# A two-layer hybrid decoder trunk: another opening order in the mixer, another order of the three passes, constant products at the start, the last scalings on one engine

## The chip, the cores and the metric

The kernel runs on one core of a Trainium2 chip. Work is done by TensorE (PE, matrix products, with a separate row PEld for loading its stationary operand), VectorE (DVE), ScalarE (ACT) and GpSimd (POOL); SyncE (SP) issues nearly all transfers. Each engine takes its instructions in the order in which they were written, and waits on semaphores for the others.

The metric is the device time of one execution in microseconds (us); less is better. Times "in the trace" count from the start of the profiled span.

## The reference

Two layers over a sequence of 512 positions of width 1024, float32. Each layer adds half of a gated feed-forward block, then a mixer of two branches (an attention in "stick-breaking" form with 4 heads of 128, and a state-space model with 24 heads of 64), then half of a second feed-forward block. A normalisation stands ahead of every block and at the end.

```python
for l in range(DEPTH):
    x = x + 0.5 * swiglu(rms_norm(x, ffn1_norm[l]), ffn1_w_up[l], ffn1_w_down[l])
    h = rms_norm(x, mix_norm[l])
    proj = h @ w_in[l]
    q, k, v, z, xbc, dt_raw, gate_sb, gate_ssm = jnp.split(proj, IN_SPLITS, axis=-1)
    y_sb = stick_breaking_attention(q, k, v) @ w_branch_sb[l]
    y_ssm = mamba2_mixer(z, xbc, dt_raw, ...) @ w_branch_ssm[l]
    merged = jax.nn.sigmoid(gate_sb) * y_sb + jax.nn.sigmoid(gate_ssm) * y_ssm
    x = x + merged @ w_out[l]
    x = x + 0.5 * swiglu(rms_norm(x, ffn2_norm[l]), ffn2_w_up[l], ffn2_w_down[l])
return rms_norm(x, final_norm)
```

The attention scores of a query block come from q and k; v enters only in the last product of a head.

## The kernel before

**Layout.** The activations stand transposed: the width of 1024 is cut into 8 blocks of 128 partitions, each 512 positions long (tiles of 128x512). A product of such an input with one weight "unit" (8 blocks of 128x128, 512 KB) gives one 128x512 result in a PSUM tile `mm`.

**Products in three passes.** Inputs and weights are float32 and are split into a high and a low part of the type float32r (hi + lo). `mm3` (L219) multiplies hi by hi, then the weight's hi by the input's lo, then the weight's lo by the input's hi, all into the same PSUM tile. `dense` (L225) does this for the 8 blocks of a unit: 8 triples, 24 products. In the rows of a profile or of an order, `mm<-hlo,whi` is a product whose moving operand is the input's low part `hlo` and whose stationary operand is the weight's high part `whi`.

**Weights.** `fetch` (L178) loads a unit into one of three raw buffers, `convert` (L184) makes the high part on ScalarE and the low part on VectorE (`wlo`, L199; for the first two units on GpSimd). `unit_order` (L77) lists the units in the order in which they are used; `unit` (L202) starts the conversion two units ahead.

**Order of the work.** The program is written by hand as one stream. Each dense triple ends in a `tick` (L153), which advances all side tasks (generators) that are due; a `yield n` in a side task says how many ticks later it goes on. So what an engine does, and in which order, is fixed when the program is built.

**Norms without waiting.** A block of the network starts with products of the input that is not yet scaled by its norm, since the norm needs the sum of squares over all 8 blocks: `norm_square` (L340) squares on ScalarE and adds on VectorE or GpSimd, `norm_end` (L357) sums over partitions with a product by ones (L363) on TensorE, and the scale `rs` follows on ScalarE and VectorE. Results of unscaled products ("not normed") are multiplied by `rs` afterwards (`scaled`, L376). Meanwhile `scale_blocks` (L260) scales the input blocks on VectorE (L265), and at one unit `project(..., swap=True)` (L238) makes the new high and low parts of the scaled input (`swapped`, L251; low part at L257); all later products use those.

**The opening of the mixer** (`mixer`, L862): the first three units are q, k and v of head 0, all from the unscaled input, with the swap at the third. Then, for each head, `qkv` (L526) starts a side task `qkv_parts` (L533) for each of the three results and one for `attention` (L561). `qkv_parts` scales an unscaled result into a tile `raw`; for v it then transposes it on TensorE (`transposed`, L518, products with the identity into a PSUM tile `pt`), and splits the result into a high and a low part (tiles `yt`). A scaled q or k is split straight from PSUM. `attention` begins with the score products of q and k (tile `pa`), which read the split parts. The heads follow as q, k, v.

**The ends.** `build` (L957) loads the first weight unit and the 8 input blocks, sets the constants, and starts. At its end the 8 blocks are scaled by the last `rs` (L999), three of them on GpSimd and five on VectorE, and stored (L1000).

Of the kernel before, what the change touches and what calls it, by code (L numbers as in the profile page):

```python
# [11 lines left out]
ALU = mybir.AluOpType  # L12
# [4 lines left out]
P = 128  # L17
SEQ = 512
NT = SEQ // P
DM = 1024  # L20
KB = DM // P
DEPTH = 2
SBH = 4
# [52 lines left out]

def unit_order(layer):  # L77
# [44 lines left out]
class Builder:  # L122
# [96 lines left out]
    def mm3(self, ps, a, b, start, stop, **kw):  # L219
        mm = self.nc.tensor.matmul  # L220
        mm(ps, a[0], b[0], start=start, stop=False, **kw)  # L221
        mm(ps, a[0], b[1], start=False, stop=False, **kw)  # L222
        mm(ps, a[1], b[0], start=False, stop=stop, **kw)  # L223
# [302 lines left out]
    def qkv(self, layer, h, first):  # L526
        parts = {}
        for t in "qkv":
            ps, normed = first[t] if first is not None else self.project(layer, t, h)
            self.spawn(self.qkv_parts(t, ps, normed, parts))  # L530
        self.spawn(self.attention(h, parts))

    def qkv_parts(self, t, ps, normed, parts):  # L533
# [11 lines left out]
        yield 2  # L545
# [316 lines left out]
    def mixer(self, layer):  # L862
# [4 lines left out]
        first = {}  # L867
        for t in "qkv":
            while t == "v" and self.scaled_blocks < KB // 2:
                self.tick()  # L870
            first[t] = self.project(layer, t, 0, swap=t == "v")
        xd, self.xd = self.xd, None
        self.xpool.__exit__(None, None, None)
        with ExitStack() as mix:
# [17 lines left out]
            with tc.tile_pool(name=f"mp{layer}", bufs=2, reuse_waits="tile") as self.mp:  # L892
# [64 lines left out]
    def build(self):  # L957
# [15 lines left out]
        self.consts()  # L973
        self.norm_start()
# [18 lines left out]
        with tc.tile_pool(name="fin", bufs=KB, reuse_waits="tile") as self.fin:  # L993
            self.xg = []
            self.ffn(DEPTH - 1, 2, self.pars[DEPTH - 1][:, G_FFN2:G_FFN2 + KB], None)
            self.flush()
            for m in range(KB):
                eng = nc.gpsimd if m in (1, 4, 7) else nc.vector
                eng.tensor_tensor(self.xg[m], self.xg[m], self.rs, op=ALU.mult)  # L999
                nc.sync.dma_start(self.out[m], self.xg[m])  # L1000
# [102 lines left out]
```

## Time and profile before

| | |
|---|---|
| device time, median of 3 runs | 2706.88 us (2706.11 to 2707.74) |
| the profiled execution | 2707.11 us, its span 2705.3 us |
| mean granted TensorE clock | 0.995 |
| busy: TensorE, VectorE, ScalarE, GpSimd | 2659.8, 1361.5, 1098.8, 316.2 us |
| moved to and from HBM | 261.43 MB read, 12.68 MB written |

How to read rows of the profile: in the timeline a row has the start, the duration, the engine, the line of the kernel, the operation, output<-inputs, the shape, the count of merged instructions, and in brackets the idle time before it with what ended it. In a list of waits a row has who waited for whom, the total, how often and the longest. In a table of windows a row has the window, its length, the busy time (and instructions) of PE, PEld, DVE, ACT and POOL, the granted TensorE clock, the share of the DMA engines and the GB/s. Products are pipelined: a row shows 0.39 us for one, while the next starts 0.23 us after it.

### The profile page before, as it was taken

Reading aid. Unit: us, or ns where it says so; the run is one execution under the profiler, and the core shown is the slowest. Engines: PE = TensorE matmul, PEld = TensorE weight load, DVE = VectorE, ACT = ScalarE, POOL = GpSimd, SP = SyncE. Lnnn points to the kernel's source line nnn. Section 1 sums busy time; section 2 is a strip of 40 time slices with the busy share of each in tenths; the row PEclk is TensorE's granted clock in tenths of the full one; section 3 lists DMA queues with packets and bytes.
Section 4 is the critical chain, followed back from the end, with each engine's and each line's share of the span. In section 5 each row is a group of like instructions: output and inputs, shape, how many; then the busy total and the mean of one; then the engine's idle time right before and its main releaser. Section 6 shows DMA issues by size and latency. Waiting matters only on the chain.

```text
span 2705.3 us, 31140 instructions
## 1 busy us (share of the span) xinstructions
PE 2659.8 (98%) x12248; PEld 2209.4 (82%) x12248; DVE 1361.5 (50%) x1933; ACT 1098.8 (41%) x1825; POOL 316.2 (12%) x479
## 2 busy tenths in 40 slices
PE   8999999999999999999999999999999999999997
PEld 6888878888888888888878888788888888788886
DVE  6333375565665464333553333755666745733333
ACT  5222246655564243222432223566555543422223
POOL 1000011132232010000100000112232410100001
PEclk9999999999999999999999999999999999999999
DMA  4322242233324423322232322323333243222322
GB/s 141 101 94 98 90 126 72 90 113 108 107 95 131 137 86 102 100 95 99 89 101 95 99 95 95 117 72 106 104 112 109 95 137 119 95 100 95 100 92 72
DMA packets 85539, 276.14 MB, mean 102 GB/s; under 512 B 10080, under 2 KB 10336, under 8 KB 85392
## 3 DMA queue, kind: packets, MB, share of 16 engines
q1 hardware_dynamic: 85104, 274.08, 30.9%
q8 instruction: 96, 1.57, 0.2%
q14 instruction: 51, 0.42, 0.1%
q10 hardware_dynamic: 288, 0.07, 0.0%
HBM read 261.43 MB, written 12.68 MB: 101 GB/s over the span
## 4 chain that ended last, share of the span: by engine, by line
PE 91%; DVE 6%; ACT 2%; issue 1%; DMA 0%; POOL 0%; DVEq 0%; SPq 0%; ACTq 0%
PE mm L221 28%; PE mm L222 28%; PE mm L223 28%; PE pt L523 1%; PE pa L765 1%; DVE wlo L199 1%; DVE tt L265 1%; DVE hlo L257 1%; PE pa L603 1%; PE pa L767 1%; PE pt L750 1%; ACT whi L195 1%; DVE cv L667 1%; PE pt L748 1%; DVE x L265 0%
## 5 line engine op out<-in xcount | busy, mean ns | idle before, releaser
L221 PE MATMUL mm<-hhi,whi 128*128 128x512 f32 x2512 | 1003.9, 400 | 6.2 <-ACT hhi L335 6.2
L222 PE MATMUL mm<-hlo,whi 128*128 128x512 f32 x2512 | 982.5, 391 | 7.0 <-DVE hlo L257 6.8
L223 PE MATMUL mm<-hhi,wlo 128*128 128x512 f32 x2512 | 982.7, 391 | 0.0
L195 ACT CAST whi<-wraw 128x1024 fp32r<-128x1024 f32 (+2 forms) x476 | 476.2, 1001 | 842.1 <-PE mm L222 517.1
L199 DVE TENSOR_TENSOR wlo<-wraw,whi 128x1024 fp32r<-128x1024 f32 (+2 forms) x472 | 586.6, 1243 | 393.5 <-ACT whi L195 392.6
L222 PEld LDWEIGHTS mm<-hlo,whi 128*128 128x128 f32 x2512 | 474.1, 189 | 105.3 <-DVE hlo L257 11.0
L223 PEld LDWEIGHTS mm<-hhi,wlo 128*128 128x128 f32 x2512 | 473.1, 188 | 100.8
L221 PEld LDWEIGHTS mm<-hhi,whi 128*128 128x128 f32 x2512 | 474.0, 189 | 98.7 <-ACT hhi L335 6.2
L223 PE MATMUL mm<-act,wlo 128*128 128x512 f32 x704 | 274.0, 389 | 0.0
L222 PE MATMUL mm<-act,whi 128*128 128x512 f32 x704 | 274.0, 389 | 0.0
L221 PE MATMUL mm<-act,whi 128*128 128x512 f32 x704 | 274.0, 389 | 0.0
L355 POOL TENSOR_TENSOR acc<-acc,sq 128x512 f32<-128x512 f32 x36 | 47.8, 1328 | 1551.9 <-ACT sq L348 1551.9
L412 DVE SCALAR_TENSOR_TENSOR x<-mm,x 128x512 f32<-128x512 f32 x96 | 66.1, 689 | 230.9 <-PE mm L223 230.9
L390 ACT ACTIVATE g<-mm 128x512 f32<-128x512 f32 x79 | 47.2, 598 | 311.2 <-PE mm L223 311.2
L404 DVE TENSOR_TENSOR a<-mm,g 128x512 f32<-128x512 f32 x88 | 60.7, 690 | 209.6 <-PE mm L223 209.6
L667 DVE SCALAR_TENSOR_TENSOR cv<-mm,conv,cv 128x511 f32<-128x511 f32 (+2 forms) x192 | 142.6, 743 | 34.8 <-ACT cv L664 33.2
L223 PEld LDWEIGHTS mm<-act,wlo 128*128 128x128 f32 x704 | 132.2, 188 | 27.5
L222 PEld LDWEIGHTS mm<-act,whi 128*128 128x128 f32 x704 | 132.2, 188 | 27.4
L221 PEld LDWEIGHTS mm<-act,whi 128*128 128x128 f32 x704 | 132.2, 188 | 27.3
L283 DVE TENSOR_TENSOR act<-a,act 128x512 fp32r<-128x512 f32 x88 | 60.9, 692 | 60.3 <-ACT act L278 60.3
L737 ACT ACTIVATE dec<-cumb,tok 128x128 f32<-128x128 f32 x192 | 62.9, 392 | 38.9 <-PE pa L765 38.9
L221 PE MATMUL mm<-yt,whi 128*128 128x512 f32 x192 | 74.9, 390 | 0.0
(208 smaller groups left out, 2451.4 us busy)
## 6 DMA issues: line engine op xcount, KB each, us to landing
wraw<-in_wflat_dram SPq DMA_DIRECT2D x394, 512.0 KB, 3.3
wraw<-in_wflat_dram SPq DMA_DIRECT2D x64, 384.0 KB, 3.1
cumb<-cum_d SPq DMA_DIRECT2D x16, 768.0 KB, 4.1
xd<-x SPq DMA_DIRECT2D x16, 256.0 KB, 4.0
wraw<-in_wflat_dram SPq DMA_DIRECT2D x16, 256.0 KB, 3.1
x<-xd SPq DMA_DIRECT2D x16, 256.0 KB, 5.2
gd<-gs SPq DMA_DIRECT2D x12, 256.0 KB, 2.1
gd<-gm SPq DMA_DIRECT2D x12, 256.0 KB, 2.0
```

The costliest lines, as they stand in the source:

```text
L195: nc.scalar.copy(hi[:, ps], raw[:, ps])
L199: eng.tensor_tensor(lo[:, ps], raw[:, ps], hi[:, ps].bitcast(F32), op=ALU.subtract)
L221: mm(ps, a[0], b[0], start=start, stop=False, **kw)
L222: mm(ps, a[0], b[1], start=False, stop=False, **kw)
L223: mm(ps, a[1], b[0], start=False, stop=stop, **kw)
L283: self.nc.vector.tensor_tensor(lo, src, hi.bitcast(F32), op=ALU.subtract)
L355: eng.tensor_tensor(self.acc, self.acc, sq, op=ALU.add)
L390: nc.scalar.activation(g, pg, AF.Silu)
L404: self.nc.vector.tensor_tensor(a, pu, g, op=ALU.mult)
L412: self.nc.vector.scalar_tensor_tensor(x, pd, 0.5, x, op0=ALU.mult, op1=ALU.add)
L667: nc.vector.scalar_tensor_tensor(u[:, i:], ps[:, :SEQ - i], tap[KCONV - 1 - i], u[:, i:], op0=ALU.mult, op1=ALU.add)
L737: nc.scalar.activation(dec[:, i, :], cumb[:, i, span(c)], AF.Relu, scale=-1.0, bias=tok[:, c, 32 + h0 + i:33 + h0 + i])
```

## The change

Four edits:

1. `qkv_order`, a new function, sets the order of the projections: q0, k0, q1, v0, k1, v1, then q, k, v of heads 2 and 3, with `dt` after head 2. The first three, from the unscaled input, are now q0, k0, q1; the swap is at q1. v0 comes fourth, from the scaled input, and is copied on ScalarE instead of scaled. The weights are laid out in that order.
2. For every v the transposes come four ticks after the result is in `raw` instead of two.
3. `mm3` multiplies by the input's low part last.
4. Eleven products of the constant `ones` with itself (128x128, into a PSUM tile nobody reads) stand ahead of the first norm, and all eight last scalings are on VectorE.

```diff
+def qkv_order():
+    yield from (("q", 0), ("k", 0), ("q", 1), ("v", 0), ("k", 1), ("v", 1))
+    for h in range(2, SBH):
+        yield from (("q", h), ("k", h), ("v", h))
+        if h == SBH - 2:
+            yield "dt", None
@@ unit_order
-    for h in range(SBH):
-        for t in "qkv":
-            yield (layer, t, h), KB
-        if h == SBH - 2:
-            yield (layer, "dt"), KB
+    for t, h in qkv_order():
+        yield ((layer, "dt") if t == "dt" else (layer, t, h)), KB
@@ mm3
         mm(ps, a[0], b[0], start=start, stop=False, **kw)
-        mm(ps, a[0], b[1], start=False, stop=False, **kw)
-        mm(ps, a[1], b[0], start=False, stop=stop, **kw)
+        mm(ps, a[1], b[0], start=False, stop=False, **kw)
+        mm(ps, a[0], b[1], start=False, stop=stop, **kw)
@@ qkv_parts (the function qkv is gone)
-        yield 2
+        yield 4 if t == "v" else 2
@@ mixer
-        first = {}
-        for t in "qkv":
-            while t == "v" and self.scaled_blocks < KB // 2:
+        first = []
+        order = list(qkv_order())
+        for i in range(3):
+            while i == 2 and self.scaled_blocks < KB // 2:
                 self.tick()
-            first[t] = self.project(layer, t, 0, swap=t == "v")
+            first.append(self.project(layer, *order[i], swap=i == 2))
...
-                for h in range(SBH):
-                    self.qkv(layer, h, first if h == 0 else None)
-                    if h == SBH - 2:
+                parts = [{} for _ in range(SBH)]
+                for i, (t, h) in enumerate(order):
+                    if t == "dt":
                         self.spawn(self.dt_stage(layer, self.project(layer, "dt")[0]))
+                        continue
+                    ps, normed = first[i] if i < len(first) else self.project(layer, t, h)
+                    self.spawn(self.qkv_parts(t, ps, normed, parts[h]))
+                    if t == "k":
+                        self.spawn(self.attention(h, parts[h]))
@@ build
+        warm = self.t(self.ptr, [P, SEQ], "pt")
+        for _ in range(11):
+            nc.tensor.matmul(warm[:, :P], self.ones, self.ones, start=True, stop=True)
         self.norm_start()
...
-                eng = nc.gpsimd if m in (1, 4, 7) else nc.vector
-                eng.tensor_tensor(self.xg[m], self.xg[m], self.rs, op=ALU.mult)
+                nc.vector.tensor_tensor(self.xg[m], self.xg[m], self.rs, op=ALU.mult)
```

The order of instructions shows where this lands. First TensorE at the very start, before:

```order
L221 MATMUL mm_186<-hhi_133,whi_130 128x512
L222 MATMUL mm_186<-hlo_134,whi_130 128x512
L223 MATMUL mm_186<-hhi_133,wlo_131 128x512
L221 MATMUL mm_186<-hhi_140,whi_130 128x512
L222 MATMUL mm_186<-hlo_141,whi_130 128x512
L223 MATMUL mm_186<-hhi_140,wlo_131 128x512
```

and now (L227 to L229 are the three passes of the changed kernel):

```order
L981 MATMUL pt_130<-ones 128x128 x11
L227 MATMUL mm_198<-hhi_145,whi_142 128x512
L228 MATMUL mm_198<-hhi_145,wlo_143 128x512
L229 MATMUL mm_198<-hlo_146,whi_142 128x512
L227 MATMUL mm_198<-hhi_152,whi_142 128x512
L228 MATMUL mm_198<-hhi_152,wlo_143 128x512
L229 MATMUL mm_198<-hlo_153,whi_142 128x512
```

The constant products come first, and in each triple the product with `hlo` has moved from second to last.

Second, TensorE in the opening of the mixer of layer 0, in the fourth unit (before: q1; now: v0), from the third triple to the first score product `pa`; `pt<-ident,raw` are the transposes of v0. Before:

```order
L223 MATMUL mm_2764<-hhi_2708,wlo_2645 128x512
L523 MATMUL pt_2791<-ident,raw_2774 128x128 x4
L221 MATMUL mm_2764<-hhi_2717,whi_2644 128x512
L222 MATMUL mm_2764<-hlo_2718,whi_2644 128x512
L223 MATMUL mm_2764<-hhi_2717,wlo_2645 128x512
L221 MATMUL mm_2764<-hhi_2724,whi_2644 128x512
L222 MATMUL mm_2764<-hlo_2725,whi_2644 128x512
L223 MATMUL mm_2764<-hhi_2724,wlo_2645 128x512
L221 MATMUL mm_2764<-hhi_2731,whi_2644 128x512
L222 MATMUL mm_2764<-hlo_2732,whi_2644 128x512
L223 MATMUL mm_2764<-hhi_2731,wlo_2645 128x512
L221 MATMUL pa_2814<-yt_2785,yt_2788 128x128
```

Now:

```order
L229 MATMUL mm_2776<-hlo_2721,whi_2656 128x512
L227 MATMUL mm_2776<-hhi_2729,whi_2656 128x512
L228 MATMUL mm_2776<-hhi_2729,wlo_2657 128x512
L229 MATMUL mm_2776<-hlo_2730,whi_2656 128x512
L227 MATMUL mm_2776<-hhi_2736,whi_2656 128x512
L228 MATMUL mm_2776<-hhi_2736,wlo_2657 128x512
L229 MATMUL mm_2776<-hlo_2737,whi_2656 128x512
L227 MATMUL mm_2776<-hhi_2743,whi_2656 128x512
L228 MATMUL mm_2776<-hhi_2743,wlo_2657 128x512
L229 MATMUL mm_2776<-hlo_2744,whi_2656 128x512
L227 MATMUL pa_2821<-yt_2797,yt_2800 128x128
L228 MATMUL pa_2821<-yt_2797,yt_2801 128x128
```

The transposes are gone from here (they stand in the next unit, behind its fifth triple); the score products keep their place behind the sixth triple. Their second row reads `yt_2801`, the low part of k0.

Third, VectorE at the same place, from the last low part of the scaled input on. Before:

```order
L257 TENSOR_TENSOR hlo_2746<-x_93,hhi_2745 128x512
L384 SCALAR_TENSOR_TENSOR raw_2770<-mm_2596,rs_2650 128x512
L382 TENSOR_TENSOR raw_2772<-mm_2638,rs_2650 128x512
L382 TENSOR_TENSOR raw_2774<-mm_2683,rs_2650 128x512
L199 TENSOR_TENSOR wlo_2777<-wraw_2639,whi_2776 128x1024
L283 TENSOR_TENSOR yt_2786<-raw_2770,yt_2785 128x512
L283 TENSOR_TENSOR yt_2789<-raw_2772,yt_2788 128x512
L283 TENSOR_TENSOR yt_2806<-pt_2791,yt_2805 128x512
```

Now:

```order
L263 TENSOR_TENSOR hlo_2758<-x_93,hhi_2757 128x512
L390 SCALAR_TENSOR_TENSOR raw_2782<-mm_2608,rs_2662 128x512
L388 TENSOR_TENSOR raw_2784<-mm_2650,rs_2662 128x512
L390 SCALAR_TENSOR_TENSOR raw_2786<-mm_2695,rs_2662 128x512
L205 TENSOR_TENSOR wlo_2789<-wraw_2651,whi_2788 128x1024
L289 TENSOR_TENSOR yt_2798<-raw_2782,yt_2797 128x512
L289 TENSOR_TENSOR yt_2801<-raw_2784,yt_2800 128x512
L289 TENSOR_TENSOR yt_2804<-raw_2786,yt_2803 128x512
```

The third raw scaling is that of q1 instead of v0, and the split behind the two of q0 and k0 reads it instead of v0's transposes; the rows up to the split of k0 (`yt_2801`) stand as before.

More of the change, by code (lines that the diff above doesn't have):

```diff
@@ L524, in transposed @@
         return pt[:, :n * P].rearrange("p (c d) -> p c d", d=P)
-    def qkv(self, layer, h, first):
-        parts = {}
-        for t in "qkv":
-            ps, normed = first[t] if first is not None else self.project(layer, t, h)
-            self.spawn(self.qkv_parts(t, ps, normed, parts))
-        self.spawn(self.attention(h, parts))
     def qkv_parts(self, t, ps, normed, parts):
@@ L866, in mixer @@
         self.open_norm(self.x, gain)
-        first = {}
-        for t in "qkv":
-            while t == "v" and self.scaled_blocks < KB // 2:
+        first = []
+        order = list(qkv_order())
+        for i in range(3):
+            while i == 2 and self.scaled_blocks < KB // 2:
                 self.tick()
-            first[t] = self.project(layer, t, 0, swap=t == "v")
+            first.append(self.project(layer, *order[i], swap=i == 2))
         xd, self.xd = self.xd, None
```

## The prediction, made before the changed kernel ran

> **What bounds the kernel now.** I read the page first (busy time, then the costliest groups), then what TensorE waits for, then the timeline and the windows around each of those waits. TensorE (PE) is busy 98% of the span, and the three passes of a split product cost the same:
>
> ```profile
> PE 2659.8 (98%) x12248; PEld 2209.4 (82%) x12248; DVE 1361.5 (50%) x1933; ACT 1098.8 (41%) x1825; POOL 316.2 (12%) x479
> L223 PE MATMUL mm<-act,wlo 128*128 128x512 f32 x704 | 274.0, 389 | 0.0
> L222 PE MATMUL mm<-act,whi 128*128 128x512 f32 x704 | 274.0, 389 | 0.0
> L221 PE MATMUL mm<-act,whi 128*128 128x512 f32 x704 | 274.0, 389 | 0.0
> ```
>
> 389 ns is a pipelined length; the starts in the rows below stand 0.23 us apart, so a dense triple takes 0.68 us. The change removes no dense product, so only TensorE's idle time, its half-clock time and the end of the program can move. The list of its waits, all engines it waits for:
>
> ```profile
> PE pt L523 <- DVE raw L382: 11.2, 2, 5.6
> PE mm L222 <- DVE hlo L257: 6.8, 10, 0.9
> PE pa L603 <- ACT xz L278: 2.9, 2, 1.5
> ```
>
> Two waits of 5.6 us, one in each layer, are the transposes of the first v in the mixer. Ten waits of up to 0.9 us are chases after the low part of a freshly scaled input. The third row is late in attention, and no edit touches it. The change is worth what it does to the first two rows, plus the two ends of the program.
>
> **Start: eleven constant products.** The first products run at half speed, and the first norm ends in a sum that TensorE must wait for:
>
> ```profile
> 0.90 0.17 DVE L302 MEMSET ones<- 128x128 f32 x1 [0.90 <-PEq L1091]
> 6.19 0.79 PE L221 MATMUL mm<-hhi,whi 128*128 128x512 f32 x1 [6.19 <-ACT hhi L335]
> 11.83 0.40 PE L223 MATMUL mm<-hhi,wlo 128*128 128x512 f32 x1
> 21.75 0.69 DVE L355 TENSOR_TENSOR acc<-acc,sq 128x512 f32<-128x512 f32 x1 [0.70 <-ACT sq L348]
> 22.48 0.63 ACT L348 ACTIVATE sq<-x 128x512 f32<-128x512 f32 x1 [0.76 <-DVE acc L355]
> 23.14 0.69 DVE L355 TENSOR_TENSOR acc<-acc,sq 128x512 f32<-128x512 f32 x1 [0.70 <-ACT sq L348]
> 23.40 0.39 PE L223 MATMUL mm<-hhi,wlo 128*128 128x512 f32 x1
> 23.89 0.30 PEld L363 LDWEIGHTS pt<-acc,ones 128*128 128x128 f32 x2 [0.52 <-DVE acc L355]
> 23.89 1.13 PE L363 MATMUL pt<-acc,ones 128*128 128x512 f32 x2
> ```
>
> From 6.19 to 11.8 some eleven products take 0.43 us instead of 0.23: at most 11 x 0.20 = 2.2 us lie there. But at 23.89 TensorE waits for a sum of squares that ScalarE and VectorE build alternately, 1.39 us a block (21.75 to 23.14), each waiting only for the other. That chain needs nothing of TensorE. TensorE's last product before it would end at 23.63, so it already idles 0.26 us; arriving earlier only lengthens this wait. I take 0; the other end is the full 2.2. The constant products themselves: the row at L363 takes 1.13 us for 512 columns at full clock, so 0.28 for 128, doubled at half clock 0.57; eleven take 3.1 to 6.3 us and end between 4.3 and 7.5 (their operand is set at 1.07). Even from 7.5 the 63 products ahead of the sum (two units of 24, 15 of the third) take 14.3 us and end at 21.8, which leaves 2 us for the splits of their weights. Cover gone, they cost 7.5 - 6.2 = 1.3 us.
>
> **The pass with the input's low part last.** A chase in the second half of layer 0 (rows of TensorE):
>
> ```profile
> 1013.60 0.50 PE L222 MATMUL mm<-hlo,whi 128*128 128x512 f32 x1 [0.66 <-DVE hlo L257]
> 1014.17 0.40 PE L221 MATMUL mm<-hhi,whi 128*128 128x512 f32 x1
> 1015.34 0.50 PE L222 MATMUL mm<-hlo,whi 128*128 128x512 f32 x1 [0.77 <-DVE hlo L257]
> 1015.67 0.40 PE L223 MATMUL mm<-hhi,wlo 128*128 128x512 f32 x1
> ```
>
> VectorE's time for the low part stays; TensorE only does its (hhi,wlo) product before the wait instead of after. Of a chase the last wait counts: one product less behind it, 0.23 us. The ten waits lie in four chases, one at each feed-forward start: 4 x 0.23 = 0.9 us. Ends: 0 (the next low part then ends last) and 10 x 0.23 = 2.3. The low part of the weight is now needed 0.23 us sooner; no row above or in the list has TensorE waiting for it.
>
> **The mixer's opening.** Here the largest wait goes, and I ask what is late next. VectorE's rows, then TensorE's, of layer 0 (layer 1 has the second of the two waits of 5.6):
>
> ```profile
> 394.18 1.22 DVE L199 TENSOR_TENSOR wlo<-wraw,whi 128x1024 fp32r<-128x1024 f32 x1
> 395.32 3.09 DVE L257 TENSOR_TENSOR hlo<-x,hhi 128x512 fp32r<-128x512 f32 x5
> 398.33 0.68 DVE L384 SCALAR_TENSOR_TENSOR raw<-mm,rs 128x512 f32<-128x512 f32 x1
> 398.93 1.27 DVE L382 TENSOR_TENSOR raw<-mm,rs 128x512 f32<-128x512 f32 x2
> 400.12 1.21 DVE L199 TENSOR_TENSOR wlo<-wraw,whi 128x1024 fp32r<-128x1024 f32 x1
> 401.25 1.28 DVE L283 TENSOR_TENSOR yt<-raw,yt 128x512 fp32r<-128x512 f32 x2
> ```
>
> ```profile
> 394.24 0.39 PE L223 MATMUL mm<-hhi,wlo 128*128 128x512 f32 x1
> 400.26 1.12 PE L523 MATMUL pt<-ident,raw 128*128 128x128 f32 x4 [5.62 <-DVE raw L382]
> 404.69 0.27 PE L222 MATMUL pa<-yt,yt 128*128 128x128 f32 x1
> 404.91 0.45 PE L221 MATMUL mm<-hhi,whi 128*128 128x512 f32 x1
> ```
>
> VectorE never rests here: scaling, low parts, three raw scalings, a weight split, the splits of q0 and k0. In the changed order its queue is the same up to those splits. TensorE no longer has the four transposes after the third triple of this unit; it goes on with triples four to six, then meets the score products pa. The second of these reads the low part of k0, the second instruction of the 401.25 row, done at 402.53. So TensorE, two products further at 394.92, waits for the fourth low part (to 396.0, the first of five in 3.09 us), runs to about 397.7, does one small product, and then idles until 402.6: **a new wait of some 4.8 us takes the old one's place**. Behind it stand the rest of this unit and the whole of k1.
>
> The second pa product moves from 404.69 to 402.6, 2.1 us sooner. Two things are paid back: the transposes, and the clock.
>
> ```profile
> 421.58 0.60 PE L523 MATMUL pt<-ident,raw 128*128 128x128 f32 x4
> 421.93 0.47 PE L221 MATMUL mm<-hhi,whi 128*128 128x512 f32 x1
> 397.63:401.05 3.42, 0.79 (x5) 0.80 (x5) 3.42 (x6) 1.22 (x2) 0.00 (x0) 0.50 0.20 70
> 401.05:404.46 3.41, 3.41 (x11) 2.70 (x10) 2.09 (x4) 0.59 (x1) 0.00 (x0) 0.54 0.44 154
> 46.06:49.47 3.41, 1.73 (x6) 0.94 (x6) 3.41 (x4) 3.38 (x6) 0.68 (x1) 0.96 0.07 19
> 49.47:52.88 3.41, 3.41 (x10) 2.60 (x10) 2.73 (x6) 0.62 (x1) 0.00 (x0) 0.54 0.45 150
> ```
>
> The next v's transposes delay the product stream by 0.35 us plus a slower first product, together 0.43; v0's now cost that in k1. The clock is the column after the five engines: 0.50 and 0.54 after the wait in the mixer, so TensorE ran at half speed from 400.26 to about 404.4, 4.2 us. The last two rows show that a stretch with TensorE half busy is enough for the same. An idle 4.8 us will do it again. Half clock for 4.2 us loses 4.2 x (1 - 0.23/0.43) = 2.0 us; before, that loss lay ahead of 404.69, now it lies behind 402.6. Per layer: -2.1 + 0.4 + 2.0 = +0.3, and +0.6 for both. Ends: half clock for 3.4 us (the last row) loses 1.6, for 5.6 (the start, 6.19 to 11.8) loses 2.6; so -0.2 to +1.8 for both layers. No half clock at all is a rival.
>
> The later transposes of v1 to v3 go two triples further back. TensorE has no wait for a ScalarE copy of v in its list, so this hides nothing: 0; with the cover gone a stall of one 128x512 pass each, 0.7 us x 6. Queues of DMA issues keep their order.
>
> [...]
>
> **The end.** The eight last scalings and what issues their stores:
>
> ```profile
> 2695.09 6.30 DVE L999 TENSOR_TENSOR xg<-xg,rs 128x512 f32<-128x512 f32 x5
> 2695.14 5.10 POOL L999 TENSOR_TENSOR xg<-xg,rs 128x512 f32<-128x512 f32 x3 [7.75 <-DVE rs L373]
> 2696.93 5.33 SPq L1000 DMA_DIRECT2D out_dram<-xg  x8
> 2698.00:2699.00 1.00, 0.00 (x0) 0.00 (x0) 1.00 (x1) 0.00 (x0) 1.00 (x2) 0.50 1.04 387
> ```
>
> Together the two engines need 6.3 us for eight; VectorE alone did five of the same size in 3.09 us (395.32), 0.60 apart. Eight take 0.68 + 7 x 0.60 = 4.9 us and end at 2700.0, 1.4 sooner. The issues of the stores end at 2702.26, 0.87 after the last scaling, because two came due together; with one due every 0.6 us about half of that goes: 0.4 more. -1.8 us. Ends: -0.9, if the scalings stand 0.72 apart; -2.0, if the stores at 387 GB/s (2.1 MB, 5.4 us from about 2696.4) set the end.
>
> **Sum**, against the profiled execution of 2707.11 (span 2705.3, 1.8 around it): 0 - 0.9 + 0.6 - 1.8 = -2.1, so 2705.0. The median of the runs shown lies 0.2 below the profiled one; I say **2704.9**. Not in the sum: the half clock at 49.47 costs 1.6 us and hangs on where a chase falls; another execution may not have it.
>
> **Rivals.** (1) **Slower by pace**: three different stationary operands in turn and the same moving operand twice in succession, at each of some 3600 triples; no product before had that moving operand twice. Each nanosecond per product costs 10.8 us, so 2704.9 + 10.8 = 2715.7; it decides from 0.7 ns on. Against it: 389 ns in all three passes, though the weights of only one were the ones just used. (2) **The clock stays full** over the new wait: -1.7 instead of +0.3 a layer, 4.0 less, 2700.9. For it: the clock's windows fall where they fall; against it: the rows at 46.06. (3) **No new wait**: pa right behind triple six at 397.7 instead of 404.6, 6.9 less 0.4 a layer: 2704.9 - 0.6 - 13.0 = 2691.3. Against it: the 401.25 row, which nothing moves. (4) **The start counts**: the sum of squares comes sooner or TensorE was the later one; 2.2 less, 2702.7. Against it: the 0.52 at 23.89. (5) **The end stays**: the stores, not the scalings, set it; 2706.7.
>
> [...]
>
> **How the numbers follow.** Forecast 60% (its own range 2703.0 to 2706.6), rival 1 6%, rival 2 17%, rival 3 5%, rival 4 7%, rival 5 5%. The range 2700.6 to 2707.0 takes in rivals 2, 4 and 5 and the ends above, and leaves out 1 and 3 and some tails. 0.2% of 2706.9 is 5.4 us, about what a measurement of this kernel can tell from no change: faster means below 2701.5. That is rival 3, most of rival 2 (12%) and 3% from mixtures of 4 with short half-clock stretches: 20%. Slower is rival 1: 6%. The rest, 74%, is within.
>
> **What would show it.** The list of waits: the row at the transposes gone, in its place pa waiting for VectorE's split of k0 from raw, 2 times, nearly 5 us; ten waits for hlo of the input nearly as long as before, plus two in the mixers. Clock about 0.5 in the window behind that wait. The sum of squares released TensorE at about 23.9 as before, with a longer wait. The eight scalings in 4.9 us, no POOL row there. I am wrong if dense products stand further apart than 227 ns, if pa does not wait, or if the sum of squares releases TensorE before 23.5.

## The result, and the profile after

The changed kernel takes 2707.09 us (median of 14 runs, 2706.24 to 2709.02), the kernel before in the same comparison 2705.95 us (14 runs, 2704.55 to 2707.74). The ratio is 1.0004 with a 95% interval of 0.9996 to 1.0012: no difference that this measurement can tell, though the medians lie 1.1 us apart the wrong way. Forecast were 2704.9 and a gain of 2.1. The profiled execution took 2706.38 us, its span 2704.7.

The busy row of the page and two of the pass groups, in the changed kernel:

```profile
PE 2663.9 (98%) x12270; PEld 2212.7 (82%) x12270; DVE 1361.7 (50%) x1936; ACT 1097.8 (41%) x1827; POOL 311.8 (12%) x476
L229 PE MATMUL mm<-act,whi 128*128 128x512 f32 x704 | 273.9, 389 | 0.0
L227 PE MATMUL mm<-act,whi 128*128 128x512 f32 x704 | 273.9, 389 | 0.0
```

389 ns as before, and the starts of successive dense products stand 227 ns apart (median) in both traces, so the pace of the products has not changed (rival 1 falls). What TensorE waits for (total, times, longest):

```profile
PE mm L229 <- DVE hlo L263: 8.5, 11, 1.2
PE pa L227 <- ACT yt L284: 4.8, 2, 2.4
PE pa L228 <- DVE yt L289: 3.9, 2, 2.0
PE pa L602 <- ACT xz L284: 3.4, 2, 1.7
PE mm L228 <- POOL wlo L205: 0.9, 1, 0.9
PE mm L229 <- DVE hlo L343: 0.7, 1, 0.7
```

The 11.2 us at the transposes of v are gone. In their place pa waits twice a layer, 4.4 us together (4.8 forecast). The waits for the input's low part (`hlo`, L263) add up to 8.5 us, but two of the eleven, 1.2 us each, are those that the prediction expected in the mixers. The chases keep 6.0 of their 6.8, and all of the difference is in the first one; in each of the three later chases the two waits are as long as before, 0.7 and 0.8 us. And a row that no edit was thought to touch has grown: pa waiting for xz, late in attention, 2.9 before and 3.4 now.

The opening of the mixer in layer 0 (timeline, TensorE and VectorE):

```profile
378.06 1.10 PE L369 MATMUL pt<-acc,ones 128*128 128x512 f32 x2 [0.21 <-DVE acc L361]
...
394.46 0.50 PE L229 MATMUL mm<-hlo,whi 128*128 128x512 f32 x1 [1.24 <-DVE hlo L263]
395.94 0.39 PE L229 MATMUL mm<-hlo,whi 128*128 128x512 f32 x1
398.72 0.33 PE L227 MATMUL pa<-yt,yt 128*128 128x128 f32 x1 [2.39 <-ACT yt L284]
399.66 1.89 DVE L289 TENSOR_TENSOR yt<-raw,yt 128x512 fp32r<-128x512 f32 x3
401.00 0.47 PE L228 MATMUL pa<-yt,yt 128*128 128x128 f32 x1 [1.96 <-DVE yt L289]
```

The second score product starts 22.9 us after the norm's product by ones; in the kernel before, where that product starts at 379.86, it was 24.8: 1.9 sooner, 2.1 were forecast. The windows of the same kernel (after the five engines' busy time: clock, DMA share, GB/s), cut where the granted clock changes:

```profile
394.19:397.60 3.41, 1.87 (x7) 1.23 (x7) 3.41 (x7) 0.28 (x2) 0.00 (x0) 1.00 0.60 178
397.60:401.02 3.42, 0.34 (x2) 0.20 (x2) 3.42 (x6) 1.67 (x3) 0.00 (x0) 1.00 0.09 22
401.02:404.43 3.41, 3.41 (x11) 2.93 (x12) 0.82 (x2) 1.54 (x5) 0.29 (x1) 0.50 0.36 132
503.42:506.83 3.41, 1.57 (x8) 1.07 (x8) 1.99 (x4) 3.39 (x6) 0.29 (x1) 1.00 0.00 0
506.83:510.24 3.41, 3.41 (x12) 2.94 (x12) 3.07 (x4) 1.27 (x3) 0.69 (x1) 0.50 0.30 70
```

The half clock behind the new wait came, 3.4 us of it. But a second stretch stands at 506.83, behind the wait for xz. The kernel before has none there.

At the end the eight scalings and the issues of their stores:

```profile
2696.01 4.91 DVE L1006 TENSOR_TENSOR xg<-xg,rs 128x512 f32<-128x512 f32 x8
2696.73 4.55 SPq L1007 DMA_DIRECT2D out_dram<-xg  x8
```

4.91 us, as worked out. From the first scaling to the end of the last instruction (2704.65, and 2705.31 before) it is 8.6 us and was 10.2: -1.6.

So the trace holds three of the four terms, and the time holds no gain. A table of segments shows where it goes. It gives the time from one norm's product by ones to the next, worked out from the start of that product in each trace; "FFN1" is the stretch from the start's norm to the first mixer's, "FFN" are the three later stretches of feed-forward blocks, each with one chase. The last column has the starts of half-clock stretches behind the first 15 us and ahead of the last norm (length 3.4, or 6.8 where marked *). The rows under the first two are the kernels of the experiments.

```
kernel                      FFN1    mixer 0  mixer 1  FFN     FFN     FFN     half clock from
before                      355.98  613.42   613.48   362.25  362.23  357.24  49, 397*, 1735*
changed                     354.40  614.87   614.62   362.34  362.31  357.23  401, 507, 1739*
changed, second run         354.35  614.94   615.31   362.36  362.36  357.23  400*, 1738*, 1847
constants alone             354.47  613.68   613.82   362.22  362.20  357.21  396*, 1734*
pass order alone            353.97  613.57   613.46   362.35  362.31  357.25  395*, 1733*
mixer order alone           355.96  613.95   613.89   362.23  362.19  357.22  49, 401*, 1739*
end alone                   354.43  613.81   613.70   362.22  362.21  357.24  396*, 1734*
pass order, last old        354.18  613.80   613.88   362.02  362.00  356.99  396*, 1734*
changed, last old           355.86  614.01   613.98   362.01  362.00  356.99  49, 400*, 1738*
changed, filled             354.40  613.05   613.24   362.32  362.31  357.19  504, 1842
changed, norm first         353.82  613.28   614.11   361.03  361.02  355.89  398*, 1733*, 1842
changed, pa later           354.18  606.21   606.44   362.34  362.36  357.19  none
before, v and pa later      353.71  605.94   605.97   362.20  362.19  357.21  none
three repairs               353.70  604.73   604.93   360.96  360.93  355.91  none
```

The chases gained nothing, and the mixers of the changed kernel are 1.1 to 1.8 us longer. (FFN1 has a half-clock stretch at 49 us, which costs 1.6, in three of the fourteen profiles, that of the kernel before among them: its profiled 2707.11 us lay near the slow end of its 14 runs, and the forecast started from there.)

### The profile page after: what moved, and what is told of

Its sections match the earlier page's. It is cut to its first block, busy times and chain, and to the rows that moved or that the text cites. A ratio compares the mean times of both kernels' runs of the same rounds, so it can differ in the third digit from the quotient of the medians.

```text
span 2704.7 us, 31234 instructions
## 1 busy us (share of the span) xinstructions
PE 2663.9 (98%) x12270; PEld 2212.7 (82%) x12270; DVE 1361.7 (50%) x1936; ACT 1097.8 (41%) x1827; POOL 311.8 (12%) x476
## 3 DMA queue, kind: packets, MB, share of 16 engines
q8 instruction: 96, 1.57, 0.2%
## 4 chain that ended last, share of the span: by engine, by line
PE 90%; DVE 6%; ACT 2%; issue 1%; POOL 0%; DMA 0%; DVEq 0%; SPq 0%; ACTq 0%
PE mm L227 28%; PE mm L229 28%; PE mm L228 28%; DVE wlo L205 1%; PE pt L529 1%; PE pa L764 1%; PE pa L602 1%; DVE tt L271 1%; PE pa L766 1%; PE pt L749 1%; ACT whi L201 1%; DVE hlo L263 1%; PE pt L747 1%; DVE cv L666 0%; ACT hhi L341 0%
## 5 line engine op out<-in xcount | busy, mean ns | idle before, releaser
L227 PE MATMUL mm<-hhi,whi 128*128 128x512 f32 x2512 | 1001.9, 399 | 0.7 <-ACT hhi L341 0.6
L229 PE MATMUL mm<-hlo,whi 128*128 128x512 f32 x2512 | 982.6, 391 | 9.4 <-DVE hlo L263 8.5
L205 DVE TENSOR_TENSOR wlo<-wraw,whi 128x1024 fp32r<-128x1024 f32 (+2 forms) x472 | 586.3, 1243 | 399.0 <-ACT whi L201 397.3
L229 PEld LDWEIGHTS mm<-hlo,whi 128*128 128x128 f32 x2512 | 472.2, 188 | 115.9 <-DVE hlo L263 13.6
L227 PEld LDWEIGHTS mm<-hhi,whi 128*128 128x128 f32 x2512 | 473.1, 188 | 92.9 <-issue 1.4
L229 PE MATMUL mm<-act,whi 128*128 128x512 f32 x704 | 273.9, 389 | 0.0
L227 PE MATMUL mm<-act,whi 128*128 128x512 f32 x704 | 273.9, 389 | 0.0
L229 PEld LDWEIGHTS mm<-act,whi 128*128 128x128 f32 x704 | 132.2, 188 | 27.5
L227 PEld LDWEIGHTS mm<-act,whi 128*128 128x128 f32 x704 | 132.2, 188 | 27.5
L227 PE MATMUL mm<-yt,whi 128*128 128x512 f32 x192 | 74.9, 390 | 0.0
```

Source lines behind the costliest of these rows:

```text
L205: eng.tensor_tensor(lo[:, ps], raw[:, ps], hi[:, ps].bitcast(F32), op=ALU.subtract)
L229: mm(ps, a[0], b[1], start=False, stop=stop, **kw)
```

## Experiments: the four edits apart

Each of these is the kernel before with one edit of the change alone; the edits are those of the diff above. The kernel before took 2705.71 us on the same chip (33 runs).

**Constants alone.**

```diff
         self.consts()
+        warm = self.t(self.ptr, [P, SEQ], "pt")
+        for _ in range(11):
+            nc.tensor.matmul(warm[:, :P], self.ones, self.ones, start=True, stop=True)
         self.norm_start()
```

> The kernel before with one edit: the eleven constant products ahead of the first norm. Theory (as predicted): the sum of squares releases TensorE as before, so the first product by ones starts at 23.7 to 23.9 us, the wait ahead of it grows by about 2 us, and the time does not move (2704.5 to 2707). Rival, the start counts: the first product by ones starts 1 us or more sooner and the time falls by 1 to 2.2 us. Second theory, from the changed kernel's trace: the half-clock stretch at 49.5 us stays, since it comes from two waits for the low part in one stretch of 3.4 us, which this edit leaves.

Measured: 2706.08 us (11 runs), ratio 1.0001 (0.9992 to 1.0009). The first product by ones starts at 23.61 us, no sooner than in the earliest of the kernels with the old start (23.61 to 24.72); FFN1 and all other segments are within 0.13 us of those of the kernel with the end alone. The start is worth nothing, as forecast. The half-clock stretch at 49 us did not come in this execution, so the second expectation was wrong: it depends on more than the waits (below).

**Pass order alone.**

```diff
-        mm(ps, a[0], b[1], start=False, stop=False, **kw)
-        mm(ps, a[1], b[0], start=False, stop=stop, **kw)
+        mm(ps, a[1], b[0], start=False, stop=False, **kw)
+        mm(ps, a[0], b[1], start=False, stop=stop, **kw)
```

> The kernel before with one edit: the pass with the input's low part last. Prediction: each of the four chases at a feed-forward start ends 0.23 us sooner against the sum of squares ahead of it, 0.9 us in all. Theory formed from the trace of the changed kernel: the unit's last product now reads the weight's high part, so ScalarE's next weight cast, which waits for that tile and stands ahead of the norm's scale on ScalarE, starts 0.23 us later; the low parts then come 0.23 us later and the chase gains nothing: 0.0 to 0.1 us per chase between the product by ones ahead of it (993.29, 1355.53 and 2331.25 us before) and the first dense product after its last wait. It may take away the half clock at 49.5 us (1.6 us), because the two waits there become shorter. Time 2704 to 2706.5.

Measured: 2706.18 us (11 runs), ratio 1.0002 (0.9994 to 1.0011). The feed-forward segments with a chase are 0.10, 0.08 and 0.01 us longer than before, not 0.23 shorter. The wait for xz late in attention is 1.68 us in both layers, against 1.46 before.

**Mixer order alone** (the order, the later transposes and nothing else).

> The kernel before with one edit: the mixer's opening order q0, k0, q1, v0 with v's transposes four ticks later. Prediction: +0.3 us a layer, +0.6 in all. Theory from the changed kernel's trace: the opening gives +0.2 to +1.1 us a layer (with the half clock behind the new wait), and late in attention (products of xz near 503 to 511 us and 1845 us) a further stretch of half clock can come in one or both layers, 1.3 us each: +1.5 to +3.5 us in all, 2707.5 to 2709.5. Rival, the mixer is neutral and the loss is elsewhere: within 0.7 us of the kernel before.

Measured: 2706.69 us (11 runs), ratio 1.0003 (0.9994 to 1.0012), +1.0 between the medians. The wait for xz stays at 1.45 us, and no half clock follows it, so the +1.5 to +3.5 of the theory did not come. The mixers take 613.95 and 613.89 us; in the five kernels with the old opening they take 613.42 to 613.88, on average 613.66. That is +0.3 us a layer, the figure of the prediction, though the old opening alone spreads over 0.5 us.

**End alone.**

```diff
-                eng = nc.gpsimd if m in (1, 4, 7) else nc.vector
-                eng.tensor_tensor(self.xg[m], self.xg[m], self.rs, op=ALU.mult)
+                nc.vector.tensor_tensor(self.xg[m], self.xg[m], self.rs, op=ALU.mult)
```

> The kernel before with one edit: the eight last scalings on VectorE. Prediction: -1.8 us (scalings 1.4 sooner, issues of the stores 0.4). Theory from the changed kernel's trace: from the start of the first scaling to the end of the span 8.7 us instead of 10.2, that is -1.5 us: scalings in 4.9 us, the last issue 0.36 us after the last scaling, and 3.4 us from there to the end. Rival, the stores set the end: 9.8 us or more, less than -0.4.

Measured: 2704.40 us (11 runs), ratio 0.9998 (0.9988 to 1.0007), -1.3 between the medians; in the trace the stretch behind the last norm's product by ones is 15.26 us instead of 16.82, -1.6.

## Experiments: why the pass order gives nothing

The clue is on ScalarE. Its rows behind a norm's product by ones, in the kernel before and then in the changed one, with the product that releases them:

```profile
993.29 1.02 PE L363 MATMUL pt<-acc,ones 128*128 128x512 f32 x2
994.38 0.40 PE L222 MATMUL mm<-hlo,whi 128*128 128x512 f32 x1
994.82 1.05 ACT L195 CAST whi<-wraw 128x1024 fp32r<-128x1024 f32 x1 [4.12 <-PE mm L222]
995.77 0.68 ACT L367 ACTIVATE rs<-pt,eps 128x512 f32<-128x512 f32 x1
```

```profile
992.93 1.02 PE L369 MATMUL pt<-acc,ones 128*128 128x512 f32 x2
994.25 0.40 PE L229 MATMUL mm<-hlo,whi 128*128 128x512 f32 x1
994.69 1.05 ACT L201 CAST whi<-wraw 128x1024 fp32r<-128x1024 f32 x1 [4.13 <-PE mm L229]
995.64 0.68 ACT L373 ACTIVATE rs<-pt,eps 128x512 f32<-128x512 f32 x1
```

ScalarE casts the weight unit two ahead into the tile `whi` of the unit that is just ending, so the cast waits for that unit's last reader of `whi`, here as in 175 places (the list of waits of the changed kernel, all engines):

```profile
ACT whi L201 <- PE mm L229: 531.1, 175, 4.4
```

Before, that reader was the unit's last product but one; with the low part of the input last it is the very last. From the product by ones to the cast it was 1.53 us and is 1.76: 0.23 later. The norm's scale `rs` stands behind the cast on ScalarE, and everything that a chase chases stands behind `rs`. The product that TensorE saves in front of the wait is added at the other end of the chain.

**Pass order, last old**: the new order in all triples but the last of each unit, on the kernel before.

```diff
+        if old:
+            mm(ps, a[0], b[1], start=False, stop=False, **kw)
+            mm(ps, a[1], b[0], start=False, stop=stop, **kw)
+            return
         mm(ps, a[1], b[0], start=False, stop=False, **kw)
         mm(ps, a[0], b[1], start=False, stop=stop, **kw)
...
-            self.mm3(ps, ..., start and k == k0, stop and k == k1 - 1)
+            self.mm3(ps, ..., start and k == k0, stop and k == k1 - 1, old=k == k1 - 1)
```

> The kernel before with the changed pass order in all triples but the last of each unit, which keeps the old order, so that the weight's high part is read last by the same product as before. Theory (the cast on ScalarE waits for the unit's last reader of the high part and stands ahead of the norm's scale): the cast behind each norm's product by ones starts 0.23 us sooner than in the kernel with the new order everywhere, and each chase gains what was predicted: from the product by ones at 993 us to the next one 362.0 us instead of 362.24 before and 362.35 with the new order everywhere, the same from 1355 to 1717; about -0.9 us in all against the kernel before. Rival, the pass order is worth nothing in a chase: 362.24 or more.

Measured: 2705.32 us (11 runs) against 2705.97 (27 runs), ratio 0.9998 (0.9989 to 1.0007). The time cannot tell it, the trace can: the three chase segments take 362.02, 362.00 and 356.99 us, 0.23 to 0.25 less than before. This kernel's rows in the same view:

```profile
991.74 1.02 PE L368 MATMUL pt<-acc,ones 128*128 128x512 f32 x2
992.84 0.40 PE L223 MATMUL mm<-hlo,whi 128*128 128x512 f32 x1
993.27 1.05 ACT L195 CAST whi<-wraw 128x1024 fp32r<-128x1024 f32 x1 [4.12 <-PE mm L223]
994.22 0.69 ACT L372 ACTIVATE rs<-pt,eps 128x512 f32<-128x512 f32 x1
```

That is 1.53 us again to the cast, and the forecast 0.23 per chase is there. The rival, that the pass order is worth nothing in a chase, falls.

The same cast makes the wait for xz longer. ScalarE ahead of that wait, before and then changed:

```profile
494.50 0.41 ACT L278 CAST btok<-cumb 128x256 fp32r<-128x256 f32 x1 [0.27 <-POOL cumb L558]
494.81 1.04 ACT L195 CAST whi<-wraw 128x1024 fp32r<-128x1024 f32 x1
```

```profile
492.85 0.41 ACT L284 CAST btok<-cumb 128x256 fp32r<-128x256 f32 x1 [0.27 <-POOL cumb L557]
493.37 1.05 ACT L201 CAST whi<-wraw 128x1024 fp32r<-128x1024 f32 x1
```

The cast starts 0.31 us behind the row ahead of it, and now 0.52. From there ScalarE works without a pause until the cast into xz that TensorE waits for (506.42 before, 505.00 now), so TensorE's wait grows by as much, 1.46 to 1.69.

**Changed, last old**: the same repair on the changed kernel, and beside it the **changed kernel a second time**. The kernel before took 2705.80 us on this chip (21 runs).

> The changed kernel unchanged, a second time, on the chip of the three runs beside it. If the first measurement stands, 2707.1 within 0.6 us and +1 us against the kernel before; if it was the chip or the moment, the time is at or below the kernel before. In the trace the wait for xz late in attention is 1.69 us in both layers in any case; a half-clock stretch behind it comes in none, one or both.

> The changed kernel with the old pass order in the last triple of each unit. Theory (what was missing from the forecast is the weight's high part being let go one product later, which holds up ScalarE): the three chases gain 0.25 us each against the changed kernel, 362.0 instead of 362.3 us from one product by ones to the next; the wait for xz late in attention falls from 1.69 to 1.46 us in both layers, and no half-clock stretch follows it, 1.3 us on average in the changed kernel: -2 to -2.6 us, 2704.5 to 2705.1. Rival, the opening of the mixer alone ate the gain: within 0.9 us of the changed kernel, above 2706.2.

Measured: the changed kernel 2706.91 us (11 runs), ratio 1.0005 (0.9996 to 1.0014), again 1.1 above the kernel before. With the old order in the last triples 2705.03 us (11 runs), ratio 0.9996 (0.9987 to 1.0005), 1.9 less; the runs of the two do not overlap (2706.30 to 2709.69, and 2703.78 to 2705.83). The wait for xz is 1.46 us again:

```profile
PE pa L607 <- ACT xz L289: 2.9, 2, 1.5
```

No half clock follows it in either layer. The mixers take 614.01 and 613.98 us, against 614.94 on average over the two profiles of the changed kernel: 0.9 us a layer came from the order in the last triples. Laid side by side product by product, the four layers of the changed kernel lose 0.2 us to the wait for the low part in the opening (1.21 to 1.24 us instead of 0.97 to 1.00) and 0.23 to the wait for xz. The two that have the half-clock stretch late in attention lose 1.1 us more there, the other two nothing. The rest, up to 0.7 us either way, is where the half clock falls in the opening.

## Experiments: the wait in the mixer, and the clock

Five more variants price the new wait and its clock: three are the changed kernel with one edit, one is the kernel before with a like edit, and the last joins three repairs.

**Changed, filled**: products of no use in the new wait.

```diff
             pz = pzs[j] = self.t(self.pa, [P, SEQ], "pa")
+            if h == 0 and j == NT - 1:
+                for i in range(18):
+                    nc.tensor.matmul(pz, self.h[0][0][:, :P], self.h[0][0], start=True, stop=True)
```

> The changed kernel with 18 products (128x512, some 4.1 us) of operands at hand, put ahead of the first score product in each layer, into the same PSUM tile, which the score products then start anew: TensorE is busy over most of the new wait. Theory (the loss behind the wait is the half clock): no half clock in the 7 us behind the wait, the products there 0.23 us apart at once, -1.6 us in layer 0 and -2.2 in layer 1 where the wait ends at the same place: -3 to -4 us, 2703 to 2704. Rival, half clock does not matter or comes anyway: within 1 us of the changed kernel, 2707.1, or slower by what the filling overruns the wait.

Measured: 2703.38 us (11 runs), ratio 0.9993 (0.9984 to 1.0002), 3.7 below the changed kernel. The wait is filled, and the products behind it run at full clock:

```profile
396.20 4.27 PE L582 MATMUL pa<-hhi 128*128 128x512 f32 x18
401.00 0.33 PE L228 MATMUL pa<-yt,yt 128*128 128x128 f32 x1 [0.48 <-DVE yt L289]
401.56 0.40 PE L228 MATMUL mm<-hhi,wlo 128*128 128x512 f32 x1
401.79 0.39 PE L229 MATMUL mm<-hlo,whi 128*128 128x512 f32 x1
```

0.23 us apart at 401.56, against 0.43 in the changed kernel at that place. The half clock that moved behind the wait costs about 2 us a layer, as the prediction had it: the mixers take 613.05 and 613.24 us instead of 614.87 and 614.62, with two stretches late in attention, of 1.1 us each, instead of one. In this execution both layers have the stretch late in attention; the expectation spoke only of the 7 us behind the wait.

**Changed, pa later**: the score products of head 0 seven triples later.

```diff
         self.attention_on = True
-        yield 1
+        yield 8 if h == 0 else 1
```

> The changed kernel with the score products of head 0 put seven triples (4.8 us) later, behind work that TensorE has at hand. Theory (the new wait of 4.4 us a layer is lost time and nothing else is late there): the wait at pa goes, and with it the half clock behind it: -4.4 - 1.6 to 2.2 us a layer, -10 to -13 us, about 2695.5. Rival, the attention that now comes later is late at its end, near 503 us and 1843 us: the waits there grow by up to 4.8 us a layer, and the gain is -3 us or less.

Measured: 2689.72 us (5 runs), ratio 0.9941 (0.9929 to 0.9954), 17.4 below the changed kernel, more than the 10 to 13 expected. No row of pa waiting for q or k is left; and the row for xz late in attention is gone too, with its half clock. The mixers take 606.2 and 606.4 us, 8.6 less: 4.4 of waiting at pa, about 2 of half clock behind it, and the rest the 1.7 us of the later wait with what followed it. The expectation had missed this last part; the rival, which expected more waiting there, was wrong in sign.

**Before, v and pa later**: the same for the old order of q, k and v.

```diff
             yield from self.scaled(r, ps, scale)
-        yield 2
+        yield 11 if t == "v" and not normed else 2
...
         self.attention_on = True
-        yield 1
+        yield 8 if h == 0 else 1
```

> The kernel before, in its own order q0, k0, v0, with the transposes of the first v nine triples later and the score products of head 0 seven triples later. Theory (what counts is that TensorE meets neither before VectorE is through with the three raw scalings and the splits): the wait of 5.6 us a layer goes with the half clock behind it, -5.6 - 2.0 us a layer, -15 us, 2690.5 to 2691.5, and the mixer takes the 606.2 to 606.4 us that it takes in the changed kernel with the same delay. Rival, the changed order of q, k and v is needed for that: a wait of 2 us or more stays at the transposes or at pa, and the time is above 2695.

Measured: 2690.70 us (5 runs), ratio 0.9943 (0.9931 to 0.9956). Mixers of 605.9 and 606.0 us, no wait at the transposes of v0 or at pa, no half clock. So the changed order of q, k and v is not needed for this. What counts here is where TensorE meets the results of VectorE's queue.

**Changed, norm first**: ScalarE's two steps of the norm's scale ahead of the weight cast.

```diff
                 nc.tensor.matmul(ps, self.ones, part, start=..., stop=...)
-        yield 3
+        yield 2
```

> The changed kernel with ScalarE's two steps of a norm's scale ahead of the weight cast that waits for the unit's end (they now stand behind it), and with VectorE's three last steps ahead of that weight's low part. TensorE's order stays. Theory (the cast holds the norm's scale up, and the scale leads the chases and the mixer's opening): the scale is ready some 2.3 us sooner, the chases at 1013, 1376 and 2353 us lose their waits of 1.4 us each, the one at 45 to 49 us most of its 1.7, and the mixer's wait for the low part and for k0 together falls from 6.0 to about 3.7 us a layer: -9 to -11 us, about 2697. Rival, the scale does not lead: the waits stay and the time stays within 1 us.

Measured: 2699.68 us (11 runs), ratio 0.9977 (0.9968 to 0.9986), 7.4 below the changed kernel. ScalarE and VectorE behind the product by ones (990.94 in this trace):

```profile
992.00 0.69 ACT L373 ACTIVATE rs<-pt,eps 128x512 f32<-128x512 f32 x1 [3.43 <-PE pt L369]
992.73 0.63 ACT L374 ACTIVATE rs<-rs 128x512 f32<-128x512 f32 x1
993.26 1.03 ACT L201 CAST whi<-wraw 128x1024 fp32r<-128x1024 f32 x1
995.00 0.69 DVE L379 SCALAR_TENSOR_TENSOR rs<-acc,rs 128x512 f32<-128x512 f32 x1
```

The scale is ready at 995.69, 4.8 us after the product by ones instead of 7.3. Each of the three chase segments loses 1.3 us; of its two waits one is left, of 0.4 us. The mixers gained less than expected: TensorE loses its wait for the low part and comes to pa 1.4 us sooner (19.2 us after the product by ones instead of 20.7), the splits of q0 and k0 come sooner by the same, and pa still waits 4.3 us a layer. VectorE gives back the other 1.1 us because the weight's low part (`wlo`, L205) now stands behind the scale in its queue: in layer 0 it starts at 383.20, behind the scale's last step (381.81); in the changed kernel it started at 382.16, ahead of that step (384.74).

**Three repairs**: the changed kernel with the last triple old, pa later and the norm first.

> The changed kernel with the old pass order in a unit's last triple, the score products of head 0 seven triples later, and ScalarE's steps of a norm's scale ahead of the weight cast. If the three act on different waits they add up: 2689.7 with the delay alone, less 3 x 1.3 for the chases and 0.4 for the first, less 1.6 a layer for the low part that the mixer waits for, so 2682 to 2684. Rival, they share the same waits: 2687 or more.

Measured: 2681.79 us (4 runs), ratio 0.9910 (0.9896 to 0.9923): 24 us below the kernel before and 25 below the changed one, and slightly better than the sum expected. TensorE's busy row and the two mixers as windows:

```profile
PE 2655.5 (99%) x12270; PEld 2207.4 (82%) x12270; DVE 1361.8 (51%) x1936; ACT 1099.9 (41%) x1827; POOL 309.1 (12%) x476
377.22:981.96 604.74, 602.41 (x2951) 506.63 (x2951) 369.93 (x623) 323.22 (x623) 128.40 (x216) 1.00 0.31 106
1703.85:2308.77 604.92, 602.59 (x2950) 506.57 (x2951) 370.15 (x623) 323.15 (x623) 128.74 (x216) 1.00 0.31 106
```

The clock is full over both, and TensorE idles 2.3 us in each.

## Why the prediction was right or wrong

- **Start, 0.** Right. Full clock comes at about 5 us instead of 12, and the first product by ones still starts when ScalarE and VectorE have the sum of squares (23.66, 23.89 before). The forecast of a longer wait there was not: the time won is spent earlier, in new waits for the low parts of the weight (0.9 us, from GpSimd) and of the input (0.7).
- **Pass order, -0.9.** This is the step that failed. The prediction counted TensorE's product ahead of the wait and took the low part's arrival as given ("VectorE's time for the low part stays"). It asked whether anyone waits for the weight's low part, which is now needed sooner, but not who waits for the weight's high part, which is now let go later. ScalarE does, 175 times in the trace, and the norm's scale stands behind it. So the scale and the low parts come 0.23 us later, and the product saved in front of the wait is lost again. For the same reason the sentence that no edit touches the wait for xz failed: it grew by 0.23 us in each layer. In the changed kernel the three chase segments lose 0.1 us or nothing, and the mixers 1.0 us each against the mixer order alone, through a later opening, the wait for xz and, in two of four layers, half clock behind it: about +2.2 instead of -0.9. With the last triple old on the kernel before, the three later chases give what was forecast, 0.23 to 0.25 each.
- **Mixer, +0.6.** Right. A new wait took the old one's place (4.4 us, in two pieces around one small product; 4.8 forecast), the second score product came 1.9 us sooner (2.1 forecast), and the half clock moved behind it. The opening alone costs +0.3 us a layer in the mixers' own length; the four layers that have it without the new order in the last triples (613.89 to 614.01 us) lie above all ten of the old opening (613.42 to 613.88). Rival 2, full clock over the wait, did not occur in any of the ten layers that have this wait unfilled. Rival 3 did not either; made by hand (pa later), it is worth 15 us on the kernel before and 17 on the changed one, where it was given 13.
- **End, -1.8.** Right in kind, 0.2 too large. The scalings take 4.91 us (4.9 forecast) and the last issue comes 0.36 us behind the last scaling (half of 0.87 forecast). But from the last issue to the end of the span it is 3.4 us instead of 3.1, and in the traces the last store lands 2.3 us behind its issue instead of 2.0; why it takes longer was not followed up. The bound of -2.0 let the stores begin at about 2696.4, ahead of the first issue at 2696.93 that the prediction's own row shows.
- **The base.** The sum was made against the profiled execution of 2707.11 us, which had the half-clock stretch at 49 us that the text named; the median is 2705.95. Of the 2.2 us between forecast and result, the pass order makes about +3.1 and the end +0.2, and the base takes back 1.1.

Sum of the terms as the traces have them: 0 + 2.2 + 0.6 - 1.6 = +1.2, against +1.1 between the medians. The medians of the single edits (+0.4, +0.5, +1.0, -1.3) add up to +0.5; each is uncertain by more than half a microsecond, so they neither confirm nor contradict the split, which rests on the traces.

## What to carry to other kernels

When an operand's last use is moved, ask not only who delivers operands to the new order but who waits for the old tile to come free, and what stands behind that waiter in its queue. Here a wait of TensorE cost its length and, where a window of 3.413 us around it had TensorE busy for 54% of the time or less, 1.1 to 2.2 us more for the half clock behind it, so that 0.2 us of waiting cost more than 1 us in some layers and executions. Where a wait is due to another engine's queue, moving the meeting point a few microseconds behind work that is at hand can be worth more than reordering what is waited for: here it was 15 to 17 us against none.

## What the runs showed of the hardware

In the traces the granted clock changed only on a grid of 3.413 us. In the changed kernel the two half-clock stretches of layer 0 begin at 401.02 and 506.83, 105.81 us or 31 steps apart, and each is one step long; in the kernel before the first two begin at 49.18 and 397.34, 348.16 us or 102 steps apart. The place of the grid against the program differs from execution to execution: taken modulo 3.4133 us, the changes lie at 1.4 us in the kernel before, at 1.7 and 0.7 in the two runs of the changed kernel, and at 1.9 in that with the norm first.

In the profiles of the kernel before and of the changed one, behind the first 15 us and ahead of the last norm, six windows of this grid at full clock were followed by half clock. TensorE was busy (by the records) for 10% to 51% of them: at 45.76 (51%), 393.92 (21%) and 1731.95 (17%) before, at 397.60 (10%), 503.42 (46%) and 1735.63 (17%) in the changed kernel. None of the others was; the least busy of them had 1.87 us of work in 3.41 (at 394.19 in the changed kernel). Two more windows, each with its follower, first from the kernel with the pass order's last triple old, then from that with the norm first:

```profile
1840.01:1843.42 3.41, 1.95 (x12) 1.52 (x10) 0.80 (x2) 3.40 (x6) 0.29 (x1) 1.00 0.00 0
1843.42:1846.83 3.41, 3.04 (x14) 2.24 (x15) 3.41 (x5) 2.16 (x3) 0.69 (x1) 1.00 0.02 5
```

```profile
1838.31:1841.73 3.42, 1.86 (x9) 1.48 (x10) 2.10 (x4) 3.39 (x6) 0.29 (x1) 1.00 0.01 2
1841.73:1845.14 3.41, 3.41 (x11) 2.63 (x10) 2.88 (x5) 1.25 (x3) 0.98 (x2) 0.50 0.42 154
```

1.95 us of work in a window kept the clock, 1.86 did not. Whether there is an exact line, these windows do not show. With a wait of 1.46 us for xz no half clock followed in any of the twelve layers that have it; with 1.69 it did in five of ten, by where the grid lay. In the first run of the changed kernel that wait fell into one window in layer 0 (503.42 to 506.83, 1.57 us of work), and half clock followed; in layer 1 it fell across two (from 1841.45, 2.85 us of work, and from 1844.86, 2.13), and the clock stayed full. That is how 0.23 us of waiting brought 1.1 us of half clock into two of the four layers of the changed kernel.
